# Four products in turn for the first four up blocks, their weight sums made in DRAM during the scan

## The chip, the cores and the metric

One core of a Trainium2 chip. The metric is the time of one execution on the device, in microseconds (us). Engines: PE multiplies matrices, DVE and ACT work elementwise, POOL (GpSimd) here mostly issues DMAs, SP issues DMAs. Each engine runs its instructions in the order in which they were written. An instruction waits on semaphores for what it needs, and everything behind it on its engine waits with it.

## The reference

One decoder block on 512 tokens of width 2048, all in float32. Cut to what matters:

```
h = rms_norm(x);  z = h @ w_in                       # 2048 wide input
o_rw  = rwkv7_mix(...)                               # recurrent scan, 16 heads of 64
o_att = swa_attention(...)                           # sliding window of 128
x = x + (g_rw * (o_rw @ w_branch[:1024]) + g_att * (o_att @ w_branch[1024:])) @ w_out
u = rms_norm(x) @ w_up                               # 2048 -> 2 x 5632
c = u[t-2]*conv_w[0] + u[t-1]*conv_w[1] + u[t]*conv_w[2] + conv_b
x = x + (silu(gate half of c) * value half of c) @ w_down
```

The change concerns the second normalisation, `@ w_up`, and what is prepared for it.

## The kernel before

**Stages.** Normalisation, attention and projections up to about 280 us; the scan of the 16 heads in 8 pairs of some 98 us, with the gates' projections (`project`, L255 to L257) filling PE between the scan's own steps, up to about 1066 us; the branch projections to about 1329 us; the product with `w_out` ("o") to about 1490 us; the product with `w_up` ("up") to about 2405 us; and the product with `w_down` ("dn") to the end.

**Seven products instead of eight.** The products o, up and dn are made in the manner of Winograd: left and right operand are cut into 2 x 2 parts, and seven products of sums of parts give the four parts of the result. Every factor is split into a high and a low half in a reduced format: ACT makes the high half as a copy, and DVE the low one by subtracting it. A product takes three matmuls for each piece: high x high, high x low, low x high.

**Up.** The result is cut into 44 blocks `f`. For each there are products P1, P2, P7, P6, P5, Q4 and P3, of 24 matmuls each. The right factors come from the normalised x and are the same for all blocks: b11 (for P1), b21 (P2), t3 (P7), t2 (P6), t1 (P5), t4 (Q4) and b22 (P3), each a high and a low tile of 128 x 2048 (`split_q`, L1034 and L1035). The left factors are pieces of `w_up`, 128 x 1024 (512 KB): P1 takes w00, P2 w01, Q4 w11, P7 the sum s3 = w00 + w10, P5 the sum s1 = w10 + w11, P6 w00 + s1 and P3 that plus w01. `Block.load` has SP load the raw piece (L1054); for s3 and s1 a second DMA of POOL's queue, which waits for the first, adds the other piece on top in SBUF (L1056). `sums` makes the weights of P6 and P3 on DVE (`a += ...`, L1063). `parts` splits them (whi on ACT L1069, wlo on DVE L1070) into a ring of three pairs; raw pieces stand in one ring of six ("raw") and one of two ("a"). `prep(i + 2)` runs that for the product two places ahead of the one that `run(i)` multiplies (L1087).

**Out of PSUM.** A block has a bank with the halves X and Z, and Y in another. P1 goes to X, and P6, P5 and P3 are added on top of it, each sum being copied out on the way; P2 goes to Z. `out` copies X into the block's u (ACT, L1103) and adds Y or Z to it (DVE, L1105, L1107). For the first four blocks X after P1 is set aside as `t1` (ACT, L1096), and u = t1 + Z later. There are two tiles u, for even and odd f, so block f + 2 needs the u that block f's convolution has read (L1121 to L1129, issued a piece at a time behind the splits, from the list `later`).

**Into up.** The order is the list `steps`. The first four blocks run while the right factors are being made: P1, P2 and P7 for all four, then P6, P5, P3 and Q4 of blocks 0 and 1 in turn, then of 2 and 3, then (4, P1). After that each block has P7, P6, P2, P5, the next block's P1, Q4, P3. Between `run(0)` and `run(11)` stand by hand the second half of the normalisation (`diagonals` makes dg; `transposed`, L1018, multiplies x by it, and the scaled copies L1025 and L1027 take it out) and the sums q and splits `split_q` that give t3, t1, t2, b22 and t4. b11 and b21 are made during o's last product.

**Sums in DRAM.** The weight sums of o and dn are made ahead of time in DRAM, into `sum_d`, during attention, scan and up: SP copies one piece there (L230), and POOL's queue adds the other (L231); `sums_along` issues one such job at a time. POOL also clears a tile in every scan pair (`BAR`, L754), which the pair's matmuls L623 read, and stores the pair's output (`o_rw_d`, L784).

**Pools.** The right factors of o's products come in tiles hhi, hlo and hraw (`fetch`, `steps_of`) from a pool of three ("hhlC").

Of the kernel before, what the change touches and what calls it, by code (L numbers as in the profile page):

```python
# [134 lines left out]
def block_kernel(ctx: ExitStack, tc: tile.TileContext, d: Dims, a: dict, out: bass.AP):  # L135
# [18 lines left out]

    ident = const.tile([P, P], F32, name="ident")
# [60 lines left out]
    jobs = []  # L216
    for w in ("o", "dn"):
        for kinds in (
            (("s1", (1, 0), (1, 1)), ("s3", (0, 0), (1, 0))),
            (("s2", "s1", (0, 0)),),  # L220
            (("s4", "s2", (0, 1)),),
        ):
            jobs += [(w, k, c, q) for c in range(NB[w]) for q in range(2) for k in kinds]
    def sums_along():

        if not jobs:
            return lambda: None
        w, (n, first, second), c, q = jobs.pop(0)
        dst = sum_d[w][n][c][q]
        pin(sync.dma_start(dst, quarter(w, first, c)[q], max_dma_last_dim=4096))  # L230
        return lambda: pool.dma_start(dst, quarter(w, second, c)[q], accum_op=ALU.add, max_dma_last_dim=4096)  # L231
# [46 lines left out]
    if True:  # L278
# [188 lines left out]
        with ExitStack() as pr:  # L467
# [396 lines left out]
    hp = hps.enter_context(tc.tile_pool(name="hhlC", bufs=3, side="right", reuse_waits="tile"))  # L864
# [92 lines left out]
    def taken_out(i, acc, xr, scale, done):  # L957
        ci, tj, sign = PRODUCTS[i][4]
        last = i in (3, 4, 5, 6)
        for t in range(NT // 2):  # L960
            for e in range(NQW):
                tt = tj * NT // 2 + t
                cs = slice(ci * DH + e * S, ci * DH + (e + 1) * S)
                x = xr(tt, cs)
                if scale == 1.0:
                    dve.tensor_tensor(x, x, acc[t][e], op=ALU.add if sign > 0 else ALU.subtract)
                else:
                    dve.scalar_tensor_tensor(x, acc[t][e], sign * scale, x, op0=ALU.mult, op1=ALU.add)
                if last:
                    done(i, tt, ci * NQW + e, cs)  # L970
# [4 lines left out]
    bq = {n: [bqp.tile([P, KH, TH], F32R, name=f"{n}{i}") for i in range(2)] for n in ("b11", "b21")}  # L975
    NCC = d.D // S
# [32 lines left out]
    def transposed(tps, i, q, dg=None):  # L1009

        pss = []
        for k in range(KH):
            if k % 2 == 0:
                pss.append(tps.tile([P, 2, TH], F32, name="ps_t", tag="tp"))
            for t in range(NT // 2):
                dst, src = pss[-1][:, k % 2, t * P : (t + 1) * P], q[:, t, k * P : (k + 1) * P]
                if dg:
                    pe.matmul(dst, src, dg[t], start=True, stop=True)  # L1018
                else:
                    pe.transpose(dst, src, ident)  # L1020
        for k in range(KH):
            src, g = pss[k // 2][:, k % 2], col("n2g", i * KH + k)
            dst = q[:, 2 * k // KH, k % (KH // 2) * TH : (k % (KH // 2) + 1) * TH]
            if k % 2:
                dve.tensor_scalar(dst, src, g, None, op0=ALU.mult)  # L1025
            else:
                act.activation(dst, src, AF.Copy, scale=g)  # L1027
# [4 lines left out]
    def split_q(n, q):  # L1032
        hi, lo = (halves(x) for x in bq[n])
        act.activation(hi, q, AF.Copy)  # L1034
        dve.tensor_tensor(lo, q, hi.bitcast(F32), op=ALU.subtract)  # L1035
# [3 lines left out]


    NPRE = 4

    class Block:
# [3 lines left out]
        def __init__(self, f):  # L1047
            self.f, self.w, self.hl = f, {}, {}

        def load(self, n):  # L1050
            f, w = self.f, self.w
            at = {"p11": (0, 0), "p12": (0, 1), "a11": (0, 0), "a12": (0, 1), "s3": (0, 0), "s1": (1, 0), "a22": (1, 1)}
            w[n] = raw_tile("a11", 2) if n in ("a11", "p11") else raw_tile()
            sync.dma_start(w[n], a["w_up"][(f, *at[n])])  # L1054
            if n in ("s3", "s1"):
                pool.dma_start(w[n], a["w_up"][f, 1, int(n == "s1")], accum_op=ALU.add)  # L1056

        def sums(self, n):

            w = self.w  # L1060
            if n in ("P6", "P3"):
                t = w["a11"]
                pin(dve.tensor_tensor(t, t, w["s1" if n == "P6" else "a12"], op=ALU.add))  # L1063

        def parts(self, n):
            one = "ap"[self.f < NPRE]
            t = self.w[{"P1": one + "11", "P2": one + "12", "P7": "s3", "P6": "a11", "P5": "s1", "Q4": "a22", "P3": "a11"}[n]]
            hi, lo = (hlp.tile([P, WC], F32R, name=f"w{e}", tag=f"w{e}") for e in ("hi", "lo"))
            pin(act.activation(hi, t, AF.Copy))  # L1069
            pin(dve.tensor_tensor(lo, t, hi.bitcast(F32), op=ALU.subtract))  # L1070
            self.hl[n] = hi, lo

        def mm(self, n):
# [6 lines left out]
            ps = getattr(self, {"P2": "Z", "P7": "Y", "Q4": "Y"}.get(n, "X"))  # L1080
            start = n in ("P1", "P7") or n == "P2" and self.f >= NPRE
# [8 lines left out]
        def out(self, n):  # L1090
            X, Y, Z = self.X, getattr(self, "Y", None), self.Z
            if n == "P7":
                return
            if n == "P1" and self.f < NPRE:
                self.t1 = up.tile([P, TH], F32, name="t1", tag="t1", bufs=NPRE)
                pin(act.activation(self.t1, X, AF.Copy))  # L1096
                return

            i, j, ps, first = {"P1": (0, 0, X, True), "P2": (0, 0, Z, False), "P6": (1, 0, X, True), "P5": (1, 1, X, True),
                               "Q4": (1, 0, Y, False), "P3": (0, 1, X, True)}[n]  # L1100
            u = us[self.f % 2][:, i, 2 + j * TH : 2 + (j + 1) * TH]
            if first:
                pin(act.activation(u, ps, AF.Copy))  # L1103
                if n == "P5":
                    pin(dve.tensor_tensor(u, u, Y, op=ALU.add))  # L1105
            else:
                pin(dve.tensor_tensor(u, self.t1 if n == "P2" and self.f < NPRE else u, ps, op=ALU.add))  # L1107

# [35 lines left out]
    for f in range(NPRE, NF):  # L1144
# [5 lines left out]
    loads = [(f + e, n) for f in range(0, NPRE, 2) for n in ("p11", "p12") for e in range(2)] + [(f, "s3") for f in pre]  # L1150
    for f in range(NF):
        loads += [(f, n) for n in ("a11", "s3", "s1", "a12", "a22") if n != "s3" or f >= NPRE]
    held = {True: [], False: []}
    for f, n in loads:
        kind = n in ("p11", "a11")
        users = {"p11": ("P1",), "p12": ("P2",), "s3": ("P7",), "s1": ("P5", "P6"), "a22": ("Q4",)}.get(n, ("P3",))
# [17 lines left out]
    def prep(i, n=1):  # L1174
        if i < len(steps):
# [3 lines left out]
            B[f].parts(nm)  # L1179
            some_later(n - 1)  # L1180
            ready.add((f, nm))
            issue_loads()
        else:
            some_later(n)

    def run(i):
        f, n = steps[i]
        prep(i + 2, 2 if 3 * NPRE <= i < 7 * NPRE else 1)
        B[f].mm(n)
        if n != "P2" or f >= NPRE:  # L1190
            B[f].out(n)
# [5 lines left out]
        if n == ("Q4" if f < NPRE else "P3"):  # L1197
# [3 lines left out]
    with tc.tile_pool(name="sqp", bufs=1, side="right", reuse_waits="tile") as sqp:  # L1201
# [3 lines left out]
        for i in range(len(PRODUCTS)):  # L1205
# [6 lines left out]
            for c in range(NB["o"]):  # L1212
                steps_of("o", i, acc[nm], c, hp)
                if last and c == NB["o"] - 4:
                    transposed(tps, 0, q11)
                    split_q("b11", q11)
                if last and c == NB["o"] - 3:
                    transposed(tps, 1, q21)
                    split_q("b21", q21)
            if last:  # L1220
                issue_loads()
                prep(0)
                prep(1)
# [12 lines left out]
    ups = psx.enter_context(tc.tile_pool(name="upps", bufs=4, space=PSUM, reuse_waits="tile"))  # L1236
    run(0)
    dg = diagonals(1)
    run(1)
    run(2)  # L1240
    transposed(tps, 0, q12, dg)
    run(3)
    dve.tensor_tensor(q11, q11, q12, op=ALU.subtract)
    transposed(tps, 1, q22, dg)
    tpx.close()
    run(4)
    dve.tensor_tensor(q12, q22, q12, op=ALU.subtract)
    split_q("t3", q12)
    tcx.close()
    x1q.close()  # L1250
    run(5)
    run(6)
    split_q("t1", q11)
    run(7)
    upy = psx.enter_context(tc.tile_pool(name="uppy", bufs=4, space=PSUM, side="right", reuse_waits="tile"))
    run(8)
    dve.scalar_tensor_tensor(q11, q11, -1.0, q22, op0=ALU.mult, op1=ALU.subtract)
    split_q("t2", q11)
    run(9)
    run(10)  # L1260
    split_q("b22", q22)
    run(11)
    dve.scalar_tensor_tensor(q21, q11, -1.0, q21, op0=ALU.mult, op1=ALU.subtract)
    split_q("t4", q21)
    x1s.close()
    upu = upx.enter_context(tc.tile_pool(name="upu", bufs=1, side="left", reuse_waits="tile"))
    for i in range(2):
        u = upu.tile([P, 2, S + 2], F32, name=f"u{i}")
        pool.memset(u[:, :, 0:2], 0.0)
        us.append(u)  # L1270
    upcx = ExitStack()
    upc = upcx.enter_context(tc.tile_pool(name="upc", bufs=1, side="right", reuse_waits="tile"))
    hp0 = upcx.enter_context(tc.tile_pool(name="hhl0", bufs=1, side="right", reuse_waits="tile"))
    for f in range(2):
        B[f].out("P2")
    for i in range(3 * NPRE, len(steps)):
        run(i)
        if steps[i] in ((2, "P6"), (2, "Q4")):
            B[2 + (steps[i][1] == "Q4")].out("P2")
# [106 lines left out]
```

## Time and profile before

| | us |
|---|---|
| median of 3 runs | 2828.68 (2828.16 to 2832.68) |
| the profiled execution | 2830.7 |
| its span, first to last instruction | 2828.9 |
| PE busy | 2774.4 (98% of the span) |
| DVE busy | 1987.5 (70%) |
| ACT busy | 1342.1 (47%) |
| POOL busy | 225.1 (8%) |

The mean granted TensorE clock was 0.996 of full speed. "Busy" is the time in which the engine has an instruction running; issuing DMAs counts for POOL and for nobody else. A stage in which PE is busy throughout has nothing to gain from the other engines, and what PE idles or runs at a lower clock is what a change of order can win.

### The profile page before, as it was taken

To read this page: it belongs to the slowest core of one execution; us is meant where nothing else is said; L and a number is where in the kernel's file an instruction comes from. 1 tells how busy PE (TensorE), PEld (TensorE's weight loads), DVE (VectorE), ACT (ScalarE), POOL (GpSimd) and SP (SyncE) were. 2 spreads that over 40 slices of the span, in tenths; PEclk is the share of its full clock that TensorE was granted. 3 is DMA by queue.
4 is the path that set the end of the run, shared out by engine and by line. 5 is a ranking of instruction groups with operands and counts; after the bars stand their busy time and mean duration, and the time that the engine had idled before them with its cause. 6 is when DMAs were issued, how large, how long until landed. Compare 5 with 4: busy or idle time off the path is not lost.

```text
span 2828.9 us, 45923 instructions
## 1 busy us (share of the span) xinstructions
PE 2774.4 (98%) x17450; PEld 2403.0 (85%) x17450; DVE 1987.5 (70%) x3437; ACT 1342.1 (47%) x2256; POOL 225.1 (8%) x299
## 2 busy tenths in 40 slices
PE   7999999999999999999999899999999999999999
PEld 5777777777777777888888899999999999888887
DVE  4588677777777774545678777878787878655555
ACT  4355445444544553322465455555545555444444
POOL 0001000000000001011010011011101110000000
PEclk9999999999999999999999999999999999999999
DMA  7865766666666667878777789888988897877775
GB/s 216 227 159 163 187 167 168 175 164 158 175 162 171 160 165 223 234 248 292 237 251 211 210 235 241 229 229 227 241 236 222 228 242 228 315 245 241 256 256 190
DMA packets 223726, 607.04 MB, mean 215 GB/s; under 512 B 24448, under 2 KB 44560, under 8 KB 222480
## 3 DMA queue, kind: packets, MB, share of 16 engines
q1 hardware_dynamic: 156096, 432.64, 47.1%
q0 software_dynamic: 36064, 132.14, 24.5%
q10 hardware_dynamic: 31344, 39.31, 4.0%
q8 instruction: 137, 2.24, 0.3%
q14 instruction: 85, 0.70, 0.1%
HBM read 554.38 MB, written 174.40 MB: 258 GB/s over the span
## 4 chain that ended last, share of the span: by engine, by line
PE 87%; DVE 5%; ACT 3%; DMA 2%; issue 1%; SPq 0%; POOL 0%; ACTq 0%; DVEq 0%; POOLq 0%
PE X L1087 18%; PE X L954 11%; PE acc L256 9%; PE acc L255 9%; PE acc L257 9%; PE Y L954 9%; PE Y L1087 9%; PE Z L1087 4%; DVE wlo L241 1%; PE psS L740 1%; PE psG L731 1%; PE bulk L623 1%; PE bulk L673 1%; PE bulk L534 1%; ACT whi L240 1%
## 5 line engine op out<-in xcount | busy, mean ns | idle before, releaser
L255 PE MATMUL acc<-xhi,whi 128*128 128x512 f32 x1152 | 462.9, 402 | 1.9 <-DVE xlo L301 1.9
L257 PE MATMUL acc<-xhi,wlo 128*128 128x512 f32 x1152 | 463.8, 403 | 0.0
L256 PE MATMUL acc<-xlo,whi 128*128 128x512 f32 x1152 | 462.2, 401 | 0.0
L947 DVE TENSOR_TENSOR wlo<-raw,whi 128x1024 fp32r<-128x1024 f32 x210 | 256.9, 1224 | 205.1 <-ACT whi L946 204.9
L240 ACT ACTIVATE whi<-raw 128x512 fp32r<-128x512 f32 x352 | 220.0, 630 | 375.7 <-PE acc L256 295.1
L946 ACT ACTIVATE whi<-raw 128x1024 fp32r<-128x1024 f32 x210 | 222.8, 1061 | 290.6 <-PE X L954 152.9
L241 DVE TENSOR_TENSOR wlo<-raw,whi 128x512 fp32r<-128x512 f32 x352 | 241.3, 689 | 167.1 <-ACT whi L240 146.9
L1087 PE MATMUL X<-b,whi 128*128 128x256 f32 x1472 | 270.2, 284 | 2.3 <-DVE u L1107 0.9
L1087 PE MATMUL X<-t,whi 128*128 128x256 f32 x1408 | 259.6, 285 | 10.3 <-DVE u L1107 9.8
L1070 DVE TENSOR_TENSOR wlo<-raw,whi 128x1024 fp32r<-128x1024 f32 x176 | 215.0, 1222 | 77.6 <-ACT whi L1069 77.3
L1087 PE MATMUL Y<-t,whi 128*128 128x256 f32 x1408 | 257.1, 283 | 0.0
L255 PEld LDWEIGHTS acc<-xhi,whi 128*128 128x128 f32 x1152 | 217.6, 189 | 43.4 <-issue 2.5
L256 PEld LDWEIGHTS acc<-xlo,whi 128*128 128x128 f32 x1152 | 217.5, 189 | 41.9 <-issue 3.3
L257 PEld LDWEIGHTS acc<-xhi,wlo 128*128 128x128 f32 x1152 | 217.5, 189 | 38.3 <-issue 1.1
L1069 ACT ACTIVATE whi<-a 128x1024 fp32r<-128x1024 f32 x132 | 139.3, 1056 | 216.5 <-DVE a L1063 214.3
L1087 PEld LDWEIGHTS X<-b,whi 128*128 128x128 f32 x1472 | 230.7, 193 | 3.1 <-issue 2.4
L1087 PEld LDWEIGHTS X<-t,whi 128*128 128x128 f32 x1408 | 221.6, 194 | 10.9 <-DVE u L1107 7.2
L1087 PEld LDWEIGHTS Y<-t,whi 128*128 128x128 f32 x1408 | 219.8, 192 | 0.0
L1087 PE MATMUL X<-b,wlo 128*128 128x256 f32 x736 | 209.3, 284 | 2.1 <-DVE wlo L1070 2.1
L1070 DVE TENSOR_TENSOR wlo<-a,whi 128x1024 fp32r<-128x1024 f32 x132 | 161.7, 1226 | 67.3 <-ACT whi L1069 66.7
L1087 PE MATMUL X<-t,wlo 128*128 128x256 f32 x704 | 200.4, 285 | 0.0
L1087 PE MATMUL Y<-t,wlo 128*128 128x256 f32 x704 | 199.4, 283 | 0.0
(339 smaller groups left out, 5762.1 us busy)
## 6 DMA issues: line engine op xcount, KB each, us to landing
raw<-in_w_up_dram SPq DMA_DIRECT2D x180, 512.0 KB, 4.6
raw<-in_w_z_dram SPq DMA_DIRECT2D x288, 256.0 KB, 3.9
s_dn<-in_w_dn_dram POOLq DMA_DIRECT2D x88, 512.0 KB, 5.9
raw<-in_w_up_dram POOLq DMA_DIRECT2D x88, 512.0 KB, 8.7
raw<-s_dn SPq DMA_DIRECT2D x88, 512.0 KB, 3.8
raw<-in_w_dn_dram SPq DMA_DIRECT2D x66, 512.0 KB, 3.5
a<-in_w_up_dram SPq DMA_DIRECT2D x48, 512.0 KB, 6.9
s_dn<-in_w_dn_dram SPq DMA_DIRECT2D x44, 512.0 KB, 4.9
```

What stands on the lines that cost most here:

```text
L240: act.activation(hi, raw, AF.Copy)
L241: dve.tensor_tensor(lo, raw, hi.bitcast(F32), op=ALU.subtract)
L255: pe.matmul(acc, whi[:, j], xhi[:, k], start=first, stop=False)
L256: pe.matmul(acc, whi[:, j], xlo[:, k], start=False, stop=False)
L257: pe.matmul(acc, wlo[:, j], xhi[:, k], start=False, stop=last)
L534: pe.matmul(ps, w[:, i], ads[:, i], start=i == lo, stop=i == hi - 1)
L946: act.activation(whi, wr, AF.Copy)
L947: dve.tensor_tensor(wlo, wr, whi.bitcast(F32), op=ALU.subtract)
L954: pe.matmul(dst, l[:, q, ts], r[:, es], start=fst and j == 0, stop=lst and j == 2, skip_group_check=True)
L1069: pin(act.activation(hi, t, AF.Copy))
L1070: pin(dve.tensor_tensor(lo, t, hi.bitcast(F32), op=ALU.subtract))
L1087: pin(pe.matmul(ps, l[:, k], r[:, k], start=start and k + i == 0, stop=last and i == 2, skip_group_check=True))
```

## The change

It has four parts.

1. **Order of the first four blocks.** All four now run P1, P2, P7 and P6 in turn (16 products). Then come P5, Q4 and P3 of blocks 0 and 1, then those of 2 and 3 with (4, P7) among them, and blocks 4 and 5 interleaved; from block 6 on the order is as before. Blocks 2 and 3 are `apart`: their P5 and P3 go to Z, so that X and u are not tied to one another. DVE adds Z to `t1` right after P2, and `place` copies `t1` into u later (ACT).
2. **Sums for the first four blocks in DRAM.** s3, s1 and the weights of P6 and P3 of blocks 0 to 3 (16 tiles of 512 KB, `up_d`) are made during the scan. `up_sum` issues for each a copy and an add, both from POOL's queue, one job after each gate, three to a scan pair. The add waits for its copy, P6 for its s1 and P3 for its P6. `load` takes these pieces ready made, and neither POOL's add (L1056) nor DVE's `a += ...` (L1063) is issued for f < 4.
3. **Right factors.** b21 is split between `run(0)` and `run(1)` instead of in o's last product; `split_q` is cut into `high` and `low`, set between other steps; `prep` is called by hand up to `run(18)`, and the low half of product 1's weights stands behind o's last sums.
4. **Pool of o's right factors.** The first two chunks of o's first product use a pool of two (`hp0`), all others a pool of three on the other side (`hhlO`).

```
+    up_d = {(f, n): dram.tile([P, DH], F32, name=f"{n}_u{f}") for f in range(NPRE) for n in ("s3", "s1", "P6", "P3")}
+        up_jobs += [(t["s3"], w[0, 0], w[1, 0]), (t["s1"], w[1, 0], w[1, 1]), (t["P6"], w[0, 0], t["s1"]),
+                    (t["P3"], t["P6"], w[0, 1])]
+    def up_sum():
+        if up_jobs:
+            dst, *parts = up_jobs.pop(0)
+            for i, src in enumerate(parts):
+                pin(pool.dma_start(dst, src, accum_op=ALU.add if i else ALU.bypass, max_dma_last_dim=4096))
...
                     emit_gate()
+                    up_sum()
...
-    hp = hps.enter_context(tc.tile_pool(name="hhlC", bufs=3, side="right", reuse_waits="tile"))
+    hp0 = hps.enter_context(tc.tile_pool(name="hhlC", bufs=2, side="right", reuse_waits="tile"))
+    hp = hps.enter_context(tc.tile_pool(name="hhlO", bufs=3, reuse_waits="tile"))
-                steps_of("o", i, acc[nm], c, hp)
+                steps_of("o", i, acc[nm], c, hp0 if i == 0 and c < 2 else hp)
...
-            sync.dma_start(w[n], a["w_up"][(f, *at[n])])
-            if n in ("s3", "s1"):
+            sync.dma_start(w[n], up_d[f, n] if (f, n) in up_d else a["w_up"][(f, *at[n])])
+            if n in ("s3", "s1") and f >= NPRE:
                 pool.dma_start(w[n], a["w_up"][f, 1, int(n == "s1")], accum_op=ALU.add)
...
-            if n in ("P6", "P3"):
+            if n in ("P6", "P3") and self.f >= NPRE:
...
+            if self.f < NPRE:
+                if n == "P2":
+                    pin(dve.tensor_tensor(self.t1, self.t1, Z, op=ALU.add))
+                    return
+                if self.apart and n != "P1":
+                    if n != "P6":
+                        i, j, more = {"P5": (1, 1, (Z, Y)), "P3": (0, 1, (Z,)), "Q4": (1, 0, (Y,))}[n]
+                        u = us[self.f % 2][:, i, 2 + j * TH : 2 + (j + 1) * TH]
+                        pin(act.activation(u, X, AF.Copy))
+                        for ps in more:
+                            pin(dve.tensor_tensor(u, u, ps, op=ALU.add))
+                    return
...
+        def place(self):
+            pin(act.activation(us[self.f % 2][:, 0, 2 : 2 + TH], self.t1, AF.Copy))
...
-    steps = [(f, n) for n in ("P1", "P2", "P7") for f in pre]
-    for f in range(0, NPRE, 2):
-        steps += [(f + e, n) for e, n in ((0, "P6"), (0, "P5"), (1, "P6"), (0, "P3"), (1, "P5"), (0, "Q4"), (1, "P3"), (1, "Q4"))]
-    steps += [(NPRE, "P1")]
+    steps = [(f, n) for n in ("P1", "P2", "P7", "P6") for f in pre]
+    steps += [(0, "P5"), (1, "P5"), (0, "Q4"), (0, "P3"), (1, "Q4"), (1, "P3")]
+    steps += [(2, "P5"), (4, "P7"), (2, "Q4"), (3, "P5"), (2, "P3"), (3, "Q4"), (3, "P3")]
+    steps += [(4, "P1"), (4, "P2"), (4, "P6"), (5, "P1"), (4, "P5"), (5, "P7"), (4, "Q4"), (4, "P3")]
+    steps += [(5, "P6"), (5, "P2"), (5, "P5"), (6, "P1"), (5, "Q4"), (5, "P3")]
...
-                    split_q("b21", q21)
...
+    run(8)
+    prep(11)
+    run(9)
+    prep(12)
+    high("t2", q11)
+    run(10)
+    prep(13)
+    low("t2", q11)
...
+    prep(17)
+    pin(dve.scalar_tensor_tensor(q21, q11, -1.0, q21, op0=ALU.mult, op1=ALU.subtract))
+    run(15)
+    prep(18)
+    high("t4", q21)
+    run(16)
+    prep(19)
+    low("t4", q21)
```

POOL before, in the first scan pair (s1_dn and s3_dn are tiles of `sum_d`, gn the pair's output):

```order
L231 DMA s1_dn0_102<-in_w_dn_dram 128x1024
L231 DMA s3_dn0_124<-in_w_dn_dram 128x1024
L231 DMA s1_dn0_102<-in_w_dn_dram 128x1024
L754 MEMSET BAR_2910 64x8x64 x2
L231 DMA s3_dn0_124<-in_w_dn_dram 128x1024
L784 DMA o_rw_d0_60<-gn_4057 128x512
```

POOL after, at the same place (s3_u0, s1_u0 and P6_u0 are tiles of `up_d` for block 0; "x2" is the copy and the add):

```order
L245 DMA s3_u0_146<-in_w_up_dram 128x1024 x2
L239 DMA s1_dn0_102<-in_w_dn_dram 128x1024
L245 DMA s1_u0_147<-in_w_up_dram 128x1024 x2
L239 DMA s3_dn0_124<-in_w_dn_dram 128x1024
L245 DMA P6_u0_148<-in_w_up_dram 128x1024
L245 DMA P6_u0_148<-s1_u0_147 128x1024
L239 DMA s1_dn0_102<-in_w_dn_dram 128x1024
L768 MEMSET BAR_2926 64x8x64 x2
L239 DMA s3_dn0_124<-in_w_dn_dram 128x1024
L798 DMA o_rw_d0_60<-gn_4073 128x512
```

Six DMAs stand ahead of the clearing of BAR that did not stand there; the scan's work on the other engines keeps its order.

DVE before, where blocks 0 and 1 end and the weights of (2, P6) and (3, P6) are made (a11_15478 and a11_15577; raw_15480 and raw_15579 are the s1 pieces that POOL adds to; c0 and c1 are convolutions of blocks 0 and 1; X_15043 and t1_15068 are block 2's):

```order
L1107 TENSOR_TENSOR u1_15433<-u1_15433,Y_15338 128x256
L1063 TENSOR_TENSOR a11_15577<-a11_15577,raw_15579 128x1024
L1129 TENSOR_TENSOR c0_15677<-c0_15677,c1_15642 128x512
L1070 TENSOR_TENSOR wlo_15713<-a11_15577,whi_15712 128x1024
L1124 SCALAR_TENSOR_TENSOR c1_15716<-u1_15433,par_148,c1_15716 128x512
L1107 TENSOR_TENSOR u0_15431<-t1_15068,X_15043 128x256
L1063 TENSOR_TENSOR a11_15478<-a11_15478,raw_15483 128x1024
```

DVE after, where t2 and t4 are made (wlo_15410 and wlo_15440 are weights of (0, P6) and (1, P6); wlo_15607 and wlo_15640 those of (0, Q4) and (0, P3)):

```order
L1317 SCALAR_TENSOR_TENSOR x00_12184<-x00_12184,x11_12187 128x2048
L1088 TENSOR_TENSOR wlo_15379<-raw_15151,whi_15378 128x1024
L1088 TENSOR_TENSOR wlo_15410<-a11_15153,whi_15409 128x1024
L1088 TENSOR_TENSOR wlo_15440<-a11_15155,whi_15439 128x1024
L1055 TENSOR_TENSOR t21_14986<-x00_12184,t20_14985 128x2048
```

```order
L1343 SCALAR_TENSOR_TENSOR x10_12186<-x00_12184,x10_12186 128x2048
L1088 TENSOR_TENSOR wlo_15607<-raw_15350,whi_15606 128x1024
L1135 TENSOR_TENSOR u0_15474<-u0_15474,Y_15353 128x256
L1088 TENSOR_TENSOR wlo_15640<-raw_15382,whi_15639 128x1024
L1055 TENSOR_TENSOR t41_14988<-x10_12186,t40_14987 128x2048
```

Before, the add of block 2's P2 into u0 stands behind a sum `a11 += raw` and its split; after, no such sum stands in the first blocks' part of DVE's queue, and the low halves t21 and t41 stand behind the splits of weights for one and two products ahead.

More of the change, by code (lines that the diff above doesn't have):

```diff
@@ L222, in block_kernel @@
         ):
-            jobs += [(w, k, c, q) for c in range(NB[w]) for q in range(2) for k in kinds]
+            jobs += [(sum_d[w][n][c][q], *(quarter(w, x, c)[q] for x in (first, second)))
+                     for c in range(NB[w]) for q in range(2) for n, first, second in kinds]
     def sums_along():
@@ L227, in sums_along @@
             return lambda: None
[L228 to L231, printed above, removed]
+        dst, first, second = jobs.pop(0)
+        pin(sync.dma_start(dst, first, max_dma_last_dim=4096))
+        return lambda: pool.dma_start(dst, second, accum_op=ALU.add, max_dma_last_dim=4096)
+    def up_sum():
[3 more added lines that the diff above has]
+                pin(pool.dma_start(dst, src, accum_op=ALU.add if i else ALU.bypass, max_dma_last_dim=4096))
     def load_w(src):
@@ L1178, in prep @@
             some_later(1)
-            B[f].parts(nm)
+            lo = B[f].parts(nm)
+            if not split:
+                lo()
             some_later(n - 1)
@@ L1187, in run @@
         f, n = steps[i]
[L1188 removed]
+        if i > 4 * NPRE + 2:
+            prep(i + 2, 2 if i <= 8 * NPRE else 1)
         B[f].mm(n)
[L1190 to L1191 removed]
+        if f < NPRE and (n == "P6" if f < 2 else n == "P5"):
+            B[f].place()
+        B[f].out(n)
         if n == "P3":
@@ L1270, in block_kernel @@
         us.append(u)
+    prep(14)
+    run(12)
+    prep(15)
+    high("b22", q22)
+    run(13)
+    prep(16)
+    low("b22", q22)
+    run(14)
+    prep(17)
[6 more added lines that the diff above has]
+    low("t4", q21)
+    x1s.close()
     upcx = ExitStack()
@@ L1273, in block_kernel @@
     hp0 = upcx.enter_context(tc.tile_pool(name="hhl0", bufs=1, side="right", reuse_waits="tile"))
-    for f in range(2):
-        B[f].out("P2")
-    for i in range(3 * NPRE, len(steps)):
+    run(17)
+    prep(20)
+    run(18)
+    for i in range(4 * NPRE + 3, len(steps)):
         run(i)
-        if steps[i] in ((2, "P6"), (2, "Q4")):
-            B[2 + (steps[i][1] == "Q4")].out("P2")
         if steps[i] == (NF - 2, "P7"):
```

117 lines of the change are left out of this document (70 added, 47 removed).

## The prediction

> **What bounds the kernel now.** I read the waits of PE first, then the windows by stage, then the chain of waits around the start of up. PE is busy for 98% of the span, so only the places count where it isn't. The windows give PE's busy time behind the first comma, then PEld, DVE, ACT and POOL, the granted clock and the DMA share:
>
> ```profile
> core 0: us, PE busy (x) PEld busy (x) DVE busy (x) ACT busy (x) POOL busy (x), PEclk, DMA share, GB/s
> 1490.00:1612.00 122.00, 107.67 (x860) 106.54 (x861) 96.03 (x115) 64.09 (x86) 11.35 (x15) 0.94 0.77 210
> 1600.00:1800.00 200.00, 200.00 (x1669) 200.00 (x1669) 159.14 (x192) 102.84 (x140) 20.73 (x24) 1.00 0.85 232
> 1329.00:1489.00 160.00, 160.00 (x703) 129.16 (x703) 108.69 (x135) 87.34 (x116) 8.89 (x15) 1.00 0.74 243
> 416.00:514.00 98.00, 96.86 (x635) 77.05 (x634) 74.11 (x182) 46.95 (x105) 8.13 (x11) 1.00 0.66 166
> ```
>
> Up's steady part (1600 to 1800) and the product o (1329 to 1489) leave PE nothing to gain, a scan pair about 1.1 us in 98. The start of up loses 14.3 us in 122, and its clock is 0.94. What PE waits for between 1480 and 1610 (total, times, longest):
>
> ```profile
> PE X L1087 <- DVE u L1107: 10.7, 3, 7.0
> PE X L1087 <- DVE wlo L1070: 2.1, 1, 2.1
> PE X L1087 <- DVE x L968: 0.9, 1, 0.9
> PE X L1087 <- ACT u L1103: 0.5, 1, 0.5
> PE X L1087 <- ACT whi L1069: 0.5, 1, 0.5
> ```
>
> That is 14.7 us idle. The chain shows whence the 7.0 comes (start, length):
>
> ```profile
> 1490.52 8.86 PE X L1087 x72
> ...
> 1557.16 11.61 DMA raw<-in_w_up_dram
> 1568.79 1.24 DVE a L1063
> 1570.13 1.07 ACT whi L1069
> 1571.22 1.23 DVE wlo L1070
> 1572.45 0.66 DVE c L1124
> 1573.11 0.34 DVE u L1107
> 1573.50 14.05 PE X L1087 x96
> ...
> 1597.34 2.88 PE X L1087 x24
> ```
>
> POOL's add of block 3's s1 is issued at 1557.16 and lands 11.61 us later; DVE's `a += raw` waits for it, and in DVE's queue the split, a convolution and the add u0 = t1 + Z stand behind it. PE can't overwrite X before that add. It starts at 1573.50, and then the clock is low:
>
> ```profile
> 1520.00:1524.00 4.00, 2.88 (x13) 2.88 (x14) 4.00 (x4) 2.12 (x2) 0.15 (x2) 0.59 0.90 197
> 1573.50:1587.55 14.05, 14.05 (x98) 14.05 (x99) 10.24 (x14) 6.38 (x9) 0.87 (x1) 0.81 0.82 217
> ```
>
> 96 matmuls took 14.05 us where 4 x 2.88 = 11.52 are due.
>
> **The loss in one sum.** o's last matmul ends 0.9 us (the wait for L968) before 1490.52, at 1489.6. From there to 1597.34, where product 28 of up, (4, P1), starts, are 107.7 us. 28 products at 2.88 us make 80.6, the 64 transposing matmuls (first row below) 7.0 at 0.11 each, as they run pipelined (chain: 3.57 us for 32). The loss is 107.7 - 87.6 = 20.1 us: 14.7 idle, and 5.4 at a low clock. That is the most that parts 1 to 3 of the change can win.
>
> The prices, from groups of 1480 to 1612 (busy, mean ns of one):
>
> ```profile
> L1018 PE MATMUL ps_t<-dg,x 128*128 128x128 f32 x64 | 7.5, 275 | 0.0
> ...
> L1070 DVE TENSOR_TENSOR wlo<-raw,whi 128x1024 fp32r<-128x1024 f32 x20 | 24.3, 1221 | 5.9 <-ACT whi L1069 5.7 <-PE Y L1087 0.2
> L1063 DVE TENSOR_TENSOR a<-a,raw 128x1024 f32<-128x1024 f32 x9 | 11.0, 1218 | 1.4 <-DMA raw<-in_w_up_dram 1.4
> L1035 DVE TENSOR_TENSOR t<-x,t 128x2048 fp32r<-128x2048 f32 x4 | 9.2, 2288 | 1.2 <-ACT t L1034 1.2
> L1107 DVE TENSOR_TENSOR u<-u,Y 128x256 f32<-128x256 f32 x4 | 1.7, 417 | 0.5 <-PE Y L1087 0.5
> ...
> L1069 ACT ACTIVATE whi<-raw 128x1024 fp32r<-128x1024 f32 x20 | 20.8, 1049 | 5.7 <-PE X L1087 3.1 <-PE Y L1087 2.5
> L1034 ACT ACTIVATE t<-x 128x2048 fp32r<-128x2048 f32 x4 | 7.6, 1908 | 1.6 <-DVE x L1247 1.4
> ...
> L1103 ACT ACTIVATE u<-X 128x256 f32<-128x256 f32 x15 | 5.7, 378 | 11.6 <-PE X L1087 11.6
> ```
>
> **Part by part, the start of up.** For the first four blocks 8 of POOL's adds go, and 8 of DVE's sums at 1.22 us, 9.8 us of an engine that is busy 96 of 122. The add of 11.61 us and the queue behind it go with them: nothing of these blocks waits for POOL any more. The first such add left is block 4's s3. Its raw tile comes free when the weights of product 15 are split, during product 13 or 14, and is split itself during product 21: 7 x 2.88 = 20 us later, where the add took 11.61. So the 7.0 us and most of the 5.4 go. Against that stand four copies by `place` (ACT, 0.38 each) and four more adds of Z (DVE, 0.42 each), 1.7 us on either engine. The 0.9 us at the start goes too, since the low half of product 1 now stands behind o's sums. I laid the instructions of PE, DVE and ACT after the change one behind another in their order, with these durations, each starting when what it waits for is done. What is late next:
>
> - **dg** (second normalisation): the transposes come after two products instead of three, so PE is there at 1489.6 + 5.8 = 1495.4. Before, dg was done at 1497.2:
>
> ```profile
> 1496.70 0.48 DVE L1006 TENSOR_SCALAR dg<-ident,rq 128x128 f32<-128x128 f32 x2
> ```
>
>   One split of 1.22 stands behind o's sums now and no longer ahead of them, so dg comes at 1496.0: 0.6 us idle.
> - **t2's low half, at product 12, (0, P6).** On DVE it stands behind the split of product 13's weights. The ring of three pairs lets ACT split those only when product 10 is done. From that end run whi 1.05, wlo 1.22 and t2 2.28: 4.55 us. PE needs it one product (2.88) and one matmul (0.12) later: 1.6 us idle.
> - **t4's low half, at product 18, (0, Q4).** From the end of product 12 ACT runs u 0.38, whi 1.05, b22 1.91, two copies 0.76 and whi 1.05 (5.15), then DVE wlo 1.22, b22 2.28, wlo 1.22 and the sum for t4 2.28 (7.0), ACT t4 1.91, u 0.38 and whi 1.05 (3.34), DVE wlo 1.22 and t4 2.28 (3.5): 19.0, less some 0.08 for each of the 9 instructions that follow one on the same engine, as pipelined instructions overlap: 18.3. PE has products 13 to 17, 14.4, and one matmul: 3.8 us idle.
> - **u of block 3, at (3, Q4) and (3, P3).** The copy into u1 waits for block 1's convolution, as before; behind it come two adds of 0.42. Laid out, PE waits 1.3 and 2.0 us, and 0.4 for one split.
> - The sum is 0.6 + 1.6 + 3.8 + 3.7 = 9.7 us idle. **The clock** after the 3.8 us: in the rows it was 0.59 for 4 us behind the wait of 2.1 us for a low half, and 0.81 for 14 us behind 7.0, so 0 to 2.5 us are lost; I take 1.2, between the two rows.
>
> After the change 9.7 + 1.2 = 10.9 us are lost, where 20.1 were. The gain is 9.2. Both bounds: if the waits on t2, t4 and u overlap more than laid out, 2 us of loss remain and 18 are won; if DVE and ACT fall behind as far as they did before, nothing is.
>
> The Trainium skill has a rule for the clock ("TensorE: Matmul & The Clock Gate", What's actually happening): after an idle window of about 3.4 us the clock falls to half, and the window runs freely. By it the wait of 3.8 us would sometimes halve the clock and the waits of 2 us never; the row of 1520 to 1524, a low clock behind 2.1 us, doesn't agree with the second. The sum by it would be 9.7 plus 0 or some 2 us, within my bounds.
>
> **b21** (1.91 us on ACT, 2.28 on DVE) leaves o's last product, where PE was full anyway: no gain there. Between product 0 and 1 it hides under the normalisation's chain, and product 4 needs it, 11 us later; it costs up to 0.5 us if it delays dg, which stands before its low half on DVE. **The pools**: o's third right factor is loaded only when the branch projection's last matmul is done, at about 1329. A load of 256 KB lands in 3.8 us (row below); a chunk of o takes 160 / 28 = 5.7 us, so it is needed at 1329 + 11.4. With the splits of three factors and one weight on ACT in between, 2 to 3 us are left over: 0, at worst 3.
>
> **Part by part, the scan.** 32 DMAs join POOL's queue, six to a pair, as the order shows. POOL before, at the first pair, then what PE needs:
>
> ```profile
> 396.65 0.81 POOL L231 DMA_DIRECT2D s_dn<-in_w_dn_dram  x1 [12.90 <-DMA s_dn<-in_w_dn_dram]
> 410.73 0.81 POOL L231 DMA_DIRECT2D s_dn<-in_w_dn_dram  x1 [13.26 <-DMA s_dn<-in_w_dn_dram]
> 411.58 1.10 POOL L754 MEMSET BAR<- 64x512 f32 x2
> ...
> 428.91 2.32 PE L623 MATMUL bulk<-BAR,BKK 128*128 128x256 f32 x10
> ```
>
> ```profile
> L231 POOL DMA_DIRECT2D s_dn<-in_w_dn_dram x55 | 44.7, 813 | 598.9 <-DMA s_dn<-in_w_dn_dram 402.9 <-DMA s_dn<-s_dn 114.4 <-DVE wlo L241 20.7
> ...
> raw<-in_w_z_dram SPq DMA_DIRECT2D x169, 256.0 KB, 3.8
> s_dn<-in_w_dn_dram POOLq DMA_DIRECT2D x55, 512.0 KB, 5.6
> ```
>
> A job is 0.81 + 5.6 until the copy has landed + 0.81 = 7.2 us, and fits into the 13 us that POOL waits between two adds. Behind the waiting add stand the clearing of BAR and the store of the pair's output. BAR is cleared at 412.7 and read at 428.91: 16.2 us of slack. So POOL costs nothing. The DMA engines have more to do:
>
> ```profile
> q0 software_dynamic: 36064, 132.14, 24.5%
> ...
> 1200.00:1400.00 200.00, 199.50 (x871) 162.97 (x870) 110.22 (x160) 64.31 (x87) 17.31 (x24) 1.00 0.80 258
> ```
>
> POOL's 132.14 MB took 24.5% of the span, so 512 KB take 2.75 us of all 16; 32 take 88 us in six pairs, 588 us. The share rises from 0.66 to about 0.81. At 0.80 (1200 to 1400) PE was busy 199.50 of 200: 0, and not over 2 us.
>
> The Trainium skill speaks against this part ("SBUF — State Buffer", the trap that DVE blocks DMA): GpSimd's descriptors starve under some of DVE's instructions, and a DMA of 620 ns takes 3100. By it six issues cost 18.6 us instead of 4.9, 13.7 more, still within the slack. The row doesn't show it: 55 issues took 813 ns in the mean, with DVE busy 74 of 98.
>
> **The rivals.**
> - *The new waits eat the gain.* DVE stays busy some 86 of 113 us and every late factor holds PE. For it: two long waits in my own sum, and an ACT that serves u, weights and factors in one queue. If t4 and u cost 4 to 6 us more, 3 to 5 us are won: 2824 to 2828. Chance 0.22.
> - *All of it is won:* the factors come in time, 2 us are lost: 2828.7 - 18 = 2811. Against it: the ring of three, which no part changes. Chance 0.08.
> - *Slower: POOL's queue comes late in the scan.* If landings grow with the share, say to the 13.3 us of the longer waits above, the three jobs ahead of BAR take 3 x 14.9 = 45 us, which no longer fits beside the adds; past a lag of 16.2 us, PE waits in six pairs. At 4 us each that costs 24: 2828.7 - 9 + 24 = 2844. Over 2.5 us each it turns the sign. Against it: DMA at 0.80 and no wait. Chance 0.12.
>
> **How the numbers follow.** The profiled execution took 2830.7, 2.0 more than the median; it would become 2821.5. From the median, 2828.7 - 9.2 = 2819.5. That case has 0.58. Its own range is 2815 to 2824. A measurement can tell 0.2%, 5.7 us, from no change: 2823.0 is the bound. Of the forecast's 0.58 about 0.54 lie below, with 0.08 for all of it: 0.62 faster. Same: 0.04 and the 0.22 of the first rival, 0.25 with something given to slower. Slower 0.13. The range reaches from the full gain, 2811, to the old time with one late pool, 2831.
>
> **What the profile would show.** Right: no wait of PE over 4 us between 1485 and 1610; its waits there on the low halves of t2 and t4; (4, P1) some 6 us earlier though one product later; the scan pairs still 98 us. Wrong: PE waiting on BAR in the scan, a wait of over 6 us at Q4 or on u, or a window with half clock longer than 5 us.

## The result, and the profile after

The changed kernel is slower by 0.6%: 2846.39 us in the median of 6 runs (2843.3 to 2853.82), where the kernel before took 2829.85 (2827.61 to 2835.59). The ratio is 1.0059, 95% interval 1.0042 to 1.0076. The forecast was 2819.5, range 2811 to 2831. The profiled execution has a span of 2841.8 us, 12.9 more than before.

First, PE's matmuls of up and of o in both kernels (kind, count, shortest/median/longest in ns, start of the first and of the last); L1087 and L954 are the kernel before, L1105 and L969 the changed one:

```profile
L1087 PE MATMUL X<-b,wlo x736: 279/283/583, 1490.8 to 2403.4; 128*128 128x256 f32 x184
L954 PE MATMUL X<-wlo,hhi x128: 388/394/400, 1329.5 to 1489.2; 128*128 128x512 f32 x128
```

```profile
L1105 PE MATMUL X<-b,wlo x736: 277/283/415, 1507.6 to 2416.6; 128*128 128x256 f32 x184
L969 PE MATMUL X<-wlo,hhi x128: 388/389/500, 1349.8 to 1507.2; 128*128 128x512 f32 x128
```

o starts 20.3 us later than before. At the start of up the changed kernel is 16.8 us behind, at the end of up 13.2, at the end 12.9. So everything from o on won 7.4 us, and everything ahead of it lost 20.3. The windows say where:

```profile
core 0: us, PE busy (x) PEld busy (x) DVE busy (x) ACT busy (x) POOL busy (x), PEclk, DMA share, GB/s
418.00:516.00 98.00, 92.16 (x599) 73.25 (x598) 67.95 (x168) 45.15 (x100) 10.66 (x14) 0.97 0.77 188
...
908.00:1006.00 98.00, 96.79 (x634) 76.91 (x633) 74.03 (x181) 46.87 (x104) 8.27 (x12) 1.00 0.67 167
...
1490.00:1612.00 122.00, 112.98 (x857) 108.87 (x856) 94.10 (x117) 71.71 (x97) 4.49 (x7) 0.97 0.62 187
```

In the six scan pairs that hold the added DMAs PE is busy 92.2 to 95.3 of 98 us, where it was 95.5 in the first and 96.8 in the others; from 908 us on, with the last of them gone, it is 96.79 again. What DVE and PE of the changed kernel wait for between 320 and 910 us (total, times, longest), and then DVE's only wait for a DMA there before:

```profile
DVE kk L566 <- DMA rsb<-rsd: 19.3, 7, 5.4
...
PE psS L754 <- DVE UV L750: 12.9, 6, 4.6
```

```profile
DVE kk L552 <- DMA rsb<-rsd: 3.7, 1, 3.7
```

PE had no such wait for UV (a step of the scan, see below) before. The 3.7 us before and 5.4 of the 19.3 us after lie ahead of the first pair (kk at 320.8); in the six pairs kk waits 13.9 us, before not at all. At three of PE's six waits for UV, of 4.6, 1.5 and 1.7 us, the clock fell too:

```profile
498.36:505.19 6.83, 4.93 (x16) 4.26 (x17) 4.48 (x11) 0.00 (x0) 1.34 (x2) 0.50 0.63 145
604.17:607.59 3.42, 3.42 (x10) 2.58 (x10) 2.66 (x6) 0.22 (x1) 0.99 (x2) 0.50 0.95 125
805.56:808.97 3.41, 3.41 (x12) 2.93 (x12) 2.42 (x7) 0.22 (x1) 0.00 (x0) 0.50 0.60 161
```

At half the clock half of PE's busy time there is lost, by estimate 5.9 us. With the 12.9 us that makes 18.8 of the 20.3.

kk is a product of the next pair's preparation (`early`, `head_rows`): one number for each of the pair's two heads and 512 tokens goes from rsT to DRAM (rsd, 4 KB) and comes back spread over the partitions (rsb), both by SP's queue. The timeline of the second pair after shows the trip (start, length):

```profile
483.41 0.81 POOL L239 DMA_DIRECT2D s_dn<-in_w_dn_dram  x1 [4.39 <-DMA s_dn<-in_w_dn_dram]
483.93 0.83 POOL L245 DMA_DIRECT2D s_u<-in_w_up_dram  x1
...
486.88 0.28 DVE L346 COPY rsT<-bulk 8x128 f32<-8x128 f32 x1
487.18 0.29 SPq L348 DMA_DIRECT2D rsd<-rsT  x1
492.25 1.12 SPq L352 DMA_DIRECT2D rsb<-rsd  x2
...
498.92 0.69 DVE L566 TENSOR_TENSOR kk<-kk,rsb 128x512 f32<-128x512 f32 x1 [4.80 <-DMA rsb<-rsd]
...
499.98 0.23 DVE L750 COPY UV<-psU 64x64 f32<-64x64 f32 x1
```

and the same before:

```profile
484.90 0.28 DVE L332 COPY rsT<-bulk 8x128 f32<-8x128 f32 x1
485.20 0.29 SPq L334 DMA_DIRECT2D rsd<-rsT  x1
488.23 1.12 SPq L338 DMA_DIRECT2D rsb<-rsd  x2
492.05 0.68 DVE L552 TENSOR_TENSOR kk<-kk,rsb 128x512 f32<-128x512 f32 x1
```

From rsd's start to rsb's issue are 5.07 us, before 3.03; the second half of rsb lands 6.0 us behind its issue, before 3.2; from rsT to kk are 12.0 us, before 7.2. Ahead of rsd stand two DMAs of 512 KB on POOL's queue, issued 3.8 and 3.3 us earlier. The first of them, an add into `sum_d`, stood there before too, issued 4.8 us ahead; the second is one of the added copies. DVE has nothing to do but wait, since its order is fixed, and behind kk stands the copy UV, a step of the scan itself, for which PE waits.

BAR, the place of my slower rival, was not late: in the first pair it was cleared from 415.70 on and read at 430.83, and in no pair were fewer than 12.8 us left between the two.

At the start of up PE waits about as the working said it would:

```profile
PE Y L1105 <- DVE t L1055: 3.6, 1, 3.6
PE X L1105 <- ACT u L1125: 1.9, 1, 1.9
PE X L1105 <- DVE t L1055: 1.8, 1, 1.8
PE Y L1105 <- DVE u L1127: 1.4, 2, 1.2
```

### The profile page after: what moved, and what is told of

Its sections match the earlier page's. It is cut to its first block, busy times and chain, and to the rows that moved or that the text cites. A ratio compares the mean times of both kernels' runs of the same rounds, so it can differ in the third digit from the quotient of the medians.

```text
span 2841.8 us, 45931 instructions
## 1 busy us (share of the span) xinstructions
PE 2777.7 (98%) x17450; PEld 2406.5 (85%) x17450; DVE 1980.4 (70%) x3433; ACT 1342.8 (47%) x2260; POOL 240.2 (8%) x323
## 4 chain that ended last, share of the span: by engine, by line
PE 83%; DVE 7%; DMA 4%; ACT 3%; issue 2%; SPq 0%; ACTq 0%; POOL 0%; DVEq 0%; POOLq 0%
PE X L1105 17%; PE X L969 11%; PE acc L270 9%; PE acc L269 9%; PE acc L271 9%; PE Y L969 9%; PE Y L1105 8%; PE Z L1105 4%; DVE wlo L255 1%; DMA rsb<-rsd 1%; DMA rsd<-rsT 1%; PE psS L754 1%; PE bulk L637 1%; PE psG L745 1%; PE bulk L687 1%
## 5 line engine op out<-in xcount | busy, mean ns | idle before, releaser
L962 DVE TENSOR_TENSOR wlo<-raw,whi 128x1024 fp32r<-128x1024 f32 x210 | 256.9, 1225 | 200.2 <-ACT whi L961 195.4
L961 ACT ACTIVATE whi<-raw 128x1024 fp32r<-128x1024 f32 x210 | 222.5, 1060 | 282.4 <-PE X L969 144.1
L1088 DVE TENSOR_TENSOR wlo<-raw,whi 128x1024 fp32r<-128x1024 f32 x184 | 224.9, 1223 | 83.3 <-ACT whi L1086 83.3
L1105 PE MATMUL X<-b,whi 128*128 128x256 f32 x1472 | 270.4, 284 | 1.9 <-ACT u L1125 1.9
L1105 PE MATMUL Y<-t,whi 128*128 128x256 f32 x1408 | 258.9, 284 | 5.0 <-DVE t L1055 3.6
L1105 PE MATMUL X<-t,whi 128*128 128x256 f32 x1408 | 257.3, 283 | 1.8 <-DVE t L1055 1.8
L1105 PEld LDWEIGHTS X<-b,whi 128*128 128x128 f32 x1472 | 230.9, 193 | 2.2 <-ACT u L1125 2.1
L1086 ACT ACTIVATE whi<-a 128x1024 fp32r<-128x1024 f32 x124 | 130.9, 1056 | 204.5 <-DVE a L1081 198.0
L1105 PEld LDWEIGHTS Y<-t,whi 128*128 128x128 f32 x1408 | 220.8, 193 | 5.5 <-DVE t L1055 3.8
L1105 PEld LDWEIGHTS X<-t,whi 128*128 128x128 f32 x1408 | 219.7, 192 | 2.0 <-DVE t L1055 2.0
L1105 PE MATMUL X<-b,wlo 128*128 128x256 f32 x736 | 209.2, 284 | 0.7 <-DVE wlo L1088 0.7
L1086 ACT ACTIVATE whi<-raw 128x1024 fp32r<-128x1024 f32 x184 | 193.0, 1049 | 29.0 <-ACT whi L1086 14.8
L1105 PE MATMUL Y<-t,wlo 128*128 128x256 f32 x704 | 200.0, 284 | 0.0
L1105 PE MATMUL X<-t,wlo 128*128 128x256 f32 x704 | 199.4, 283 | 0.1
```

Source lines behind the costliest of these rows:

```text
L961: act.activation(whi, wr, AF.Copy)
L962: dve.tensor_tensor(wlo, wr, whi.bitcast(F32), op=ALU.subtract)
L1088: return lambda: pin(dve.tensor_tensor(lo, t, hi.bitcast(F32), op=ALU.subtract))
L1105: pin(pe.matmul(ps, l[:, k], r[:, k], start=start and k + i == 0, stop=last and i == 2, skip_group_check=True))
```

## The experiments

The theory after this reading: **the small round trip waits behind POOL's large DMAs, and DVE waits for it in order.** The rivals: the volume of 32 more DMAs costs PE its time wherever they lie; another part of the change does it. The kernel before took 2830.2 to 2830.3 us beside all of these runs.

**e1, the sums alone.** `up_sum` and its jobs added to the kernel before, nothing else.

```
+                    up_sum()          # behind emit_gate(), in the kernel before
```

> The kernel before with part 2's 32 DMAs alone: the sums are made in the scan at the places where the change has them, and nobody reads them. Between 320 and 1040 us the changed kernel lost 20.1 us against the kernel before (the store rsd starts the last pair at 995.19 instead of 975.09), and DVE waited 19.3 us for rsb instead of 3.7. If the DMAs alone cause it (theory: the small round trip rsT, rsd, rsb waits behind them), this kernel is slower by 18 to 22 us, some 2850, with DVE's kk waiting for rsb 15 to 20 us. If the loss comes from another part of the change (order of the instructions, pools), it stays within 3 us of the kernel before.

2849.43 us, ratio 1.0086 (1.0059 to 1.0114), and DVE's wait:

```profile
DVE kk L565 <- DMA rsb<-rsd: 17.2, 7, 4.7
```

The DMAs alone cause the loss.

**e2, the change without the sums.**

```
-                    up_sum()
...
-  sync.dma_start(w[n], up_d[f, n] if (f, n) in up_d else a["w_up"][(f, *at[n])])
+  sync.dma_start(w[n], a["w_up"][(f, *at[n])])
```

> The changed kernel without part 2's 32 DMAs: the first four blocks load raw pieces of w_up where they would load the sums, so their weights are not the sums and the output is another. All other instructions and loads are as in the changed kernel. Theory: the scan is back at 98 us a pair and only the gain at the start of up is left, 9 us less than the kernel before, some 2820 (2817 to 2823). If the scan's loss came from the other parts, it stays at about 2845.

2824.24 us, 0.9981 (0.9972 to 0.9991). The scan is as before (96.78 of 98 busy). The gain of the rest is 6.0 us and not 9, just outside the range that I had expected.

**e3, a longer trip without traffic.**

```
+                rd2 = dram.tile([2 * NT, P], F32, name="rsd2", tag="rsd2", bufs=4)
+                sync.dma_start(rd2, rd)
...
```

> The kernel before with one more copy of 4 KB in DRAM (rsd to rsd2) between rsd and rsb in each of the scan's 8 pairs: the round trip gets 2 to 3 us longer, and nothing is added to the traffic worth naming. Theory: rsb landed about 0.7 us before kk needed it, so each of the 7 pairs with a round trip beside the scan loses 1.3 to 2.3 us: 9 to 16 us, 2839 to 2846, DVE waiting for rsb. Rival (it is the volume of the DMAs, not the latency of this chain): within 3 us of the kernel before.

2830.09 us, 1.0003 (0.9993 to 1.0012): no change, so this expectation failed. The timeline tells why:

```profile
486.49 0.28 DVE L332 COPY rsT<-bulk 8x128 f32<-8x128 f32 x1
...
497.27 0.68 DVE L556 TENSOR_TENSOR kk<-kk,rsb 128x512 f32<-128x512 f32 x1
```

The trip did get longer (in this pair 4.5 us from rsd to rsb), but kk was no longer 7.2 us behind rsT but 10.8: the program that puts the instructions in order had set two products BKK and others of DVE ahead of kk, presumably because it counts the second hop. The latency as such costs nothing here; it costs where DVE's order doesn't leave room for it. That gave e5.

**e4, the sums behind the pair's store.**

```
+                stored = final(p, lt)
...
+                    with tc.issue_after(stored.ins):
+                        up_sum()
```

> The changed kernel with each pair's three sums ordered on POOL's queue behind the pair's store o_rw_d, so that they run in the 40 us ahead of the next round trip and not during it; the same 32 DMAs, the same share. Theory: rsd and rsb are as fast as before (2 us and 4 us), the scan's pairs are 98 us again and the gain at the start of up stays: 2818 to 2823, faster than both. Rival volume (any 32 DMAs more in the scan cost 20 us): 2843 to 2848. Rival POOL's queue (jobs ahead of the clearing of BAR): faster too, since they stand behind it, so e3 has to tell that one apart.

2824.95 us, 0.9982 (0.9972 to 0.9991): faster than both, though 2 us above what I had expected. POOL's queue and SP's in the second pair:

```profile
429.15 1.06 POOL L245 DMA_DIRECT2D s_u<-in_w_up_dram  x2
430.20 0.52 POOL L245 DMA_DIRECT2D P_u<-in_w_up_dram  x1
...
486.39 0.29 SPq L348 DMA_DIRECT2D rsd<-rsT  x1
488.54 1.12 SPq L352 DMA_DIRECT2D rsb<-rsd  x2
```

The copies lie 57 us ahead of the trip, and rsb is issued 2.15 us behind rsd. The pair's window:

```profile
418.00:516.00 98.00, 96.78 (x635) 76.90 (x634) 74.14 (x181) 46.85 (x104) 12.19 (x17) 1.00 0.80 198
```

The DMA share was 0.80, more than the changed kernel's 0.77, with PE busy 96.78 of 98. So it isn't the volume.

**e5, kk later on DVE.** The sums stay where the change has them; kk and what needs it move behind two products that don't.

```
+                    ahead = dve.tensor_tensor(BKK[hs, :, ol:oh], k23[hs], Ei3[hs], op=ALU.mult)
+                with tc.issue_after(ahead.ins):
+                    dve.tensor_tensor(kk, kk, rb, op=ALU.mult)
+                dve.tensor_tensor(kb, kk, ta, op=ALU.mult)
```

> The changed kernel with DVE's kk, which reads rsb, ordered behind the two products BKK of k and Ei, so that it stands some 10.8 us behind rsT on DVE where it stood 7.2 us behind it (e3 had it at 10.8 and did not wait). The 32 DMAs stay where the changed kernel has them, so the round trip stays as long, up to 12 us from rsT to kk. Theory (what costs is DVE waiting in order at kk, with the scan's copies UV behind it): the wait of 19.3 us falls to 4 to 8, and of the scan's 20 us some 13 to 16 come back: 2830 to 2834. Rival (the DMAs cost PE their time in another way, whatever DVE does): 2843 to 2848.

2822.55 us, 0.9974 (0.9964 to 0.9983), better than expected:

```profile
483.06 0.28 DVE L346 COPY rsT<-bulk 8x128 f32<-8x128 f32 x1
483.37 0.29 SPq L348 DMA_DIRECT2D rsd<-rsT  x1
...
487.84 1.12 SPq L352 DMA_DIRECT2D rsb<-rsd  x2
494.46 0.69 DVE L617 TENSOR_TENSOR kk<-kk,rsb 128x512 f32<-128x512 f32 x1
```

```profile
DVE kk L617 <- DMA rsb<-rsd: 2.1, 1, 2.1
```

The trip is still long (4.47 us from rsd to rsb), kk stands 11.4 us behind rsT, and its one wait, 2.1 us, lies ahead of the first pair (kk at 321.5). The granted clock stayed at 1.00 in the scan. All of the 20 us came back, by the order on DVE alone, and that order by itself is worth only about 1 us where no DMAs are added (e9 against e6). That settles the mechanism.

**e6, the pools alone** (part 4 in the kernel before).

```
+                steps_of("o", i, acc[nm], c, hp0 if i == 0 and c < 2 else hp)
```

> The kernel before with part 4 alone: o's right factors in hp0 for the first two chunks and in hhlO on the other side of SBUF for all others. In the traces a product of o takes 22.40 us before (1371.95 to 1394.35) and in e1, and 21.76 us in the changed kernel, e2 and e4, with the same 96 matmuls. If the place of the right factors sets it, this kernel has 21.76 us too, loses some 0.9 us in the first product (wait for the third factor), and is 2 to 4 us faster than before, 2826 to 2828. If another part sets it (b21 moved, the order), it has 22.40 us and is no faster.

2827.23 us, 0.9993 (0.9984 to 1.0002): 3.0 us in the median, but the interval still holds no change. The trace is clearer. One form of o's matmuls between 1380 and 1440 us, before and in e6 (busy, mean ns):

```profile
L954 PE MATMUL X<-whi,hhi 128*128 128x512 f32 x54 | 21.6, 399 | 0.0
```

```profile
L954 PE MATMUL X<-whi,hhi 128*128 128x512 f32 x55 | 21.4, 389 | 0.0
```

399 ns against 389; the other two forms had 392 and 394 before, and 389 in e6. A product of o takes 21.76 us instead of 22.40 (1350.24 to 1372.00 in e6).

**e7, e4 and e5 together.**

> e4 (sums behind the store) and e5 (kk later) together. Theory: e4 left 1 to 2 us in the scan (a wait of 4.9 us for rsb, most of it in the first pair), so this brings 0 to 1 us over e4: 2822 to 2826. If the volume still cost something through DVE, 2 us or more over e4.

2822.67 us, 0.9979 (0.9968 to 0.9990): 2.3 under e4 and the same as e5. By the mark that I had set, 2 us or more over e4, this would speak for the volume, but the intervals of e4 and e7 overlap widely, and e5 and e7 have the same volume. Once kk has room, it doesn't matter where the sums lie.

**e8, one copy at the trip**, in the kernel before.

```
...
+                first = pool.tensor_copy(seen, rs)
+                with tc.issue_after(first.ins):
+                    pool.dma_start(load_d.pop(0), a["w_up"][0, 0, 0], max_dma_last_dim=4096)
```

> The kernel before with one 512 KB copy from DRAM to DRAM in each scan pair, issued on POOL's queue as soon as the numbers for rsT are there (a copy of 128 x 8 on POOL waits for them), so some 2 to 3 us ahead of the store rsd: 8 DMAs instead of the 32, a quarter of the volume, all at the round trip. Theory (the small DMAs wait behind a large one in flight): rsd takes 4 to 5.5 us instead of 2, DVE waits 1 to 2.5 us at kk in each of 7 pairs, and the kernel is 7 to 14 us slower, 2837 to 2844. Rival volume (20 us for 32 DMAs): at most 5 us, 2830 to 2835.

2833.38 us, 1.0014 (1.0005 to 1.0023): 3.1 us, less than I expected and within the rival's range. DVE waits 6.5 us at kk, where the kernel before waits 3.7. The copy came out nearer to rsd than planned:

```profile
486.63 0.54 POOL L340 DMA_DIRECT2D load<-in_w_up_dram  x1 [0.27 <-issue]
...
487.05 0.29 SPq L335 DMA_DIRECT2D rsd<-rsT  x1
490.40 1.12 SPq L344 DMA_DIRECT2D rsb<-rsd  x2
```

Issued 0.4 us ahead of rsd, it left the first half of the trip at 3.35 us in this pair (2.6 to 4.1 in all seven; before 1.6 to 3.0), where the change's two DMAs, 3.3 and 3.8 us ahead, made it 5.07. How the delay depends on the number and the lead of the large DMAs is left open; taken alone this run doesn't tell theory and rival apart, e4 and e5 do.

**e9, what the start of up is worth.** The kernel before with e6's pools and e5's kk.

> The kernel before with part 4 (e6) and kk later (as in e5), with neither the new order of up's first blocks nor the sums in DRAM. It prices what is left of the change: e5 is this kernel plus parts 1 to 3. Pools 3 us, kk later 0 to 2 us (e7 against e4): 2825 to 2828. If my term for the start of up (9.2 us) were right, e5 would be 9 us faster than this one; by the traces (dn begins 908.7 to 910.4 us behind up's first product in the changed kernel, e4, e5 and e7, 910.1 to 913.7 in before, e1, e6 and e8) it is 3 to 5 us. If this one is as fast as e5, 2822.5, parts 1 to 3 are worth nothing.

2826.12 us, 0.9986 (0.9977 to 0.9995). e5 is 3.6 us faster: that is the best value here for what parts 1 to 3 bring, once the sums in DRAM cost nothing. The two intervals overlap, so it could be near nothing; in the traces, from o's last matmul to dn's first, e5 is 4.2 us faster (910.4 against 914.6). The times quoted in the expectation leave out e2, whose up was slower in its trace (915.4 us from up's first matmul to dn's), with four falls of the clock.

**e10, the low halves first**, in e5.

```
-    prep(13)
     low("t2", q11)
+    prep(13)
...
-    prep(19)
     low("t4", q21)
+    prep(19)
```

> e5 with the low halves of t2 and t4 ahead of the split of the next product's weights on DVE (two pairs of lines exchanged, nothing else moves). My working for the two waits said that they come from that place in DVE's queue: t2's wait 1.8 us goes to 0 to 0.3, t4's 3.6 falls by the 1.2 to 1.7 of the split, to some 2.0. 3 us less, and 0 to 2 more if the clock keeps up behind the shorter gap: 2817.5 to 2820. If the low halves wait for their sources instead, nothing changes: 2822 to 2823.

2817.61 us, 0.9956 (0.9943 to 0.9968): the fastest, 12.7 us under the kernel before and 4.9 under e5, in 5 runs. Two of its waits at the start of up:

```profile
PE X L1109 <- ACT u L1129: 1.8, 1, 1.8
PE Y L1109 <- DVE t L1059: 1.8, 1, 1.8
```

t2's wait is gone and t4's, 3.6 us in e5, is half, as the two chains in the prediction say; a wait for a whi grew from 0.2 to 1.0.

## Why the prediction was wrong

**The step that failed: "The share rises from 0.66 to about 0.81. At 0.80 (1200 to 1400) PE was busy 199.50 of 200: 0, and not over 2 us."** The share did rise (0.77), but in the stage I compared with nothing that PE needs hung on a late DMA (PE was idle for 0.5 us in 200). The scan has a chain through DRAM on which DVE's order hangs, and that chain had next to no room: before, kk stood 3.8 to 5.3 us behind the issue of rsb, whose second half was issued 0.5 us later and landed 3.0 to 3.2 us after that, so by estimate 0.1 to 1.6 us were left. I priced the DMAs by bandwidth, and they cost latency. The price was 20.3 us in the changed kernel, 19.2 in e1. My sign "the scan pairs still 98 us" failed: from one store rsd to the next it was 99.8 to 105.1 us in six of them.

**The slower rival** had the sign and nearly the time (2844 us), with the wrong mechanism. It took POOL's queue and BAR; what was late was a DMA of another queue. Its condition, a lag of 16.2 us, was never met, so that its time came near the measured one is luck. Two sums of the rivals don't hold either: with a gain of 9.2 us the sign turns at 1.5 us a pair, not 2.5, and 3 to 5 us won make 2824 to 2826, not 2828.

**The start of up.** The waits were right: t2 1.8 us (said 1.6), t4 3.6 (3.8), u 1.4 and 1.9 (1.3 and 2.0), and POOL's add is gone from the waits. The 0.6 for dg did not come. The gain was not right: it is 3.6 us by e9 and e5, where I had 9.2. The term of the sum that was mis-sized is the clock. It fell twice, each time for 3.41 us to 0.50, with PE busy throughout; ahead of each fall stands the row of the 3.41 us before it:

```profile
1570.15:1573.56 3.41, 0.91 (x7) 0.92 (x8) 3.41 (x4) 0.20 (x1) 0.00 (x0) 1.00 0.51 157
1573.56:1576.97 3.41, 3.41 (x18) 3.41 (x17) 0.50 (x1) 0.00 (x0) 0.00 (x0) 0.50 0.56 156
...
1604.28:1607.69 3.41, 1.52 (x13) 1.32 (x12) 2.31 (x3) 1.49 (x3) 0.86 (x1) 1.00 1.11 302
1607.69:1611.10 3.41, 3.41 (x18) 3.41 (x18) 2.64 (x3) 1.06 (x2) 0.00 (x0) 0.50 1.03 328
```

That is 1.7 us each, 3.4 in all, where I had 1.2. (4, P1) starts at 1611.6, 104.1 us behind o's last matmul, 3.6 earlier than before where I had said some 6. By the prediction's own sum 13.6 us were lost up to there and not 10.9, so 6.5 us were won. Of the 13.6, 8.7 are PE's waits (the four rows shown for the start of up) and 3.4 the clock; I can't place the other 1.5, nor 1.3 of the 5.4 us that I put down to the clock before, where its two falls make 4.1. Behind (4, P1), where the sum stopped, about 1.7 us more were lost, 0.7 of it in a wait for a wlo at 1644, among the interleaved blocks 4 and 5; up to dn's first matmul the changed kernel's trace has 4.8 us won (909.1 against 913.9). What is left to the 3.6 of the medians is within the spread of the runs: kernels with the same up as before took 910.1 to 913.7 us from up's first matmul to dn's.

**The pools** were priced at 0, at worst 3 us lost. o's first product did wait, 0.9 us, but the other six got 0.64 us shorter each, which the prediction had no term for.

## What to carry to other kernels

Before traffic is added to a stage, look there for small DMAs that an in-order engine waits for, and for the room between their landing and their reader; a share of 0.8 that is free for streams is not free for such a chain. Room is often to be had by order: two products that don't need the late operand, set ahead of the one that does, took back all 20 us. And where a wait comes from an instruction's place in a queue, two lines exchanged (e10) can be worth about as much as a new schedule.

## What the runs showed of the hardware

**Large DMAs of one queue delay small ones of another.** SP stores 4 KB and issues the reading back when the store is done. Between the two starts lay 1.6 to 3.0 us in the scan pairs of the kernel before, 1.8 to 3.5 in e4, and 4.3 to 5.4 in the six pairs of the changed kernel that hold the added DMAs. A DMA of 512 KB on POOL's queue stood ahead of the store in all three; the last one was issued 4.3 to 4.9 us ahead before and 2.3 to 3.4 us ahead in the changed kernel. With one 0.4 to 0.7 us ahead (e8) it was 2.6 to 4.1 us. Whether the lead or the number counts was not tried.

**The matmul's pace changed with two pools.** With no edit but to the pools of o's right factors, its matmuls take 389 ns in all three forms instead of 399, 392 and 394. Which address it is that counts was not tried.

**The clock falls behind short waits too.** It was 0.50 for 3.41 us from 1607.69, where PE had been busy for 1.52 of the 3.41 us ahead and the longest single wait was one of 1.9 us; in the scan it fell at 604.17 behind a wait of 1.5 us. The Trainium skill ("TensorE: Matmul & The Clock Gate", What's actually happening) lets it fall after an idle window of about 3.4 us. No wait ahead of these two falls was that long, so by the measurement shorter ones have to be counted in.
